# Gate units held behind attention and index scores, late expert units spread over the last stage, and the last outputs finished one by one

## The chip, the cores and the metric

The kernel runs on one core of a Trainium2 chip. The metric is device time in microseconds (us), the median of several executions. Names of engines here and below: PE is TensorE (matrix products), DVE is VectorE, ACT is ScalarE, POOL is GpSimd, SP is the engine whose queue issues most of the transfers.

## The reference

One layer of a streaming encoder for two groups of tokens that share weights: 256 tokens of a prompt, and 8 x 16 new tokens (the sample) with a cache of 256 past tokens each. In short:

```
mod = silu(c) W_ada + b_ada -> shift1, scale1, gate1, shift2, scale2, gate2
h = RMSNorm(x) * (1 + scale1) + shift1
P = h W_in, columns: [RWKV-7 | DSA attention + indexer | two branch gates]
branch A: RWKV-7 time mixing (16 heads of 64, a state update per token)
branch B: sparse attention: indexer I[t,s] = sum_h w[t,h] relu(q_idx[t,h].k_idx[s]),
          top-k admissible keys (k = 64 or 68 here), softmax over them
m = sigmoid(gA) * (oA W_pa) + sigmoid(gB) * (oB W_pb);  x = x + gate1 * (m W_out)
h2 = RMSNorm(x) * (1 + scale2) + shift2;  x = x + gate2 * PEER(h2)
PEER: 8 heads, 128 x 128 = 16384 experts, top 16 pairs of keys each;
      out = sum over chosen e of g_e gelu(h2 . u_e) v_e
```

All data is fp32 and D_MODEL is 1024.

## The kernel before

Products in fp32 are made of two halves: `hilo` rounds a tile to a high part (ACT, `wh`) and takes the difference as a low part (`wl`, on DVE or POOL), and a product is three matmuls, high x high, high x low and low x high. A weight tile is 512 KB (128 x 1024), is loaded by SP into a ring of four and split.

A tile scheduler sets the order on each engine; it starts from the order in which the program emits its steps. Engines run their own instructions in order and wait for one another by semaphores; `after(ins, other)` adds a wait by hand. The stages follow one another:

- **Front** (0 to some 735 us). `ORDER` is a string with a letter for each step: R is one of eight RWKV pairs (`rwkv_pair`), D a quarter of the attention heads (`dsa_quarter`), M a unit of the modulation (`mod_unit`), G one of sixteen gate units (`gate_unit`; a small g takes the low parts on POOL), I the indexer. A gate unit multiplies 24 matmuls of 128x384 (`tposp`, in the tile `mm`), takes a sigmoid on ACT and stores the result in DRAM (`d_401`) for later; nothing in the front waits for it. The indexer scores the sample (`index_s`: eight units of a key load `cki`, two matmuls into `dx`, a relu `rel` on ACT and a matmul into `bx`), then the prompt (`index_p`: matmuls into `dx`, then 8 rounds of max and replace on DVE per 128 tokens, `select`). An RWKV pair projects r, k and v (72 matmuls in `mm`), and then runs a chain of small matmuls and DVE steps. `attend_p` is the prompt's attention of a quarter, in two halves i of 128 tokens: scores `dx<-kT,qTp`, softmax, transposes of `se`, products with `vv`, and a store from `qr`.
- **Mix** (from some 733 us): the branches' outputs are loaded back from DRAM (`px`), split (`pbh`, `pbl`) and multiplied with the projections.
- **PEER choice**, then the dense half for the prompt: for 128 rows j of 128 experts, `dense_u` makes gelu(h2 . u) for all 256 prompt tokens, `weights` makes the gates (stored as `Wd`), and from 1326 us on the **v stage** multiplies them with `v` (`dense_v`, one unit per row j, all into the four outputs `bx`, `cp`, `dx`, `dx`). Every third unit is not split (`whole`: 8 matmul records on fp32 data). Rows 0 to 75 are kept in SBUF. Of the 52 late rows, 20 (76 to 95) are made beforehand and put into DRAM (`Ad`, read back as `gB`), 11 more are made beforehand and kept (`gA`), and the last 21 are made by `dense_u` inside the v stage when a place among the `gA` comes free. Late rows need their gates, loaded four rows at a time (`Ws`).
- The sample's experts are gathered row by row (`peer_sparse`, indirect transfers issued by POOL), spread by `pull(rate)` over the dense stages: a pull is two gathers, and `SR` holds the pulls per unit. A gather waits for the unit five before it (`pace`). All pulls are done by unit 122.
- **Tail**: `residual` multiplies each finished output by its gate, adds x and stores it.

Of the kernel before, what the change touches and what calls it, by code (L numbers as in the profile page):

```python
# [18 lines left out]
OP = mybir.AluOpType  # L19
# [154 lines left out]

PSB = {"mm": 2, "fx": 2, "bx": 1, "dx": 2, "cp": 1}
ALIAS = {"ix": "cp", "cs": "bx", "u": "fx"}
ORDER = "GGIggggRRDMMMGRMRDMRGMGMRMDGMMRRMGDMMMGGGMGGM"


N1, NW, NA, NB = 36, 76, 12, 20  # L180
SR, UR = (0.5, 0.4, 0.69), 0.5
S0, PH = 30, 4
WB, EB = (4, 4, 3), 5
UENG, VENG, GENG, VN = 'v', 'v', 'g', 3
SENG = 'gv'
# [7 lines left out]
class K:  # L193
# [76 lines left out]
            self.mm(p, lo[:, k, tok], wh, start=False, stop=(k == 7))  # L270
        return p

    def tposp(self, W, c, m, LT):

        hi, lo = LT
        p = self.ps([128, NT], tag="mm")[:m, :LT[0].shape[2]]
        cs = slice(c * 128, c * 128 + m)
        for k in range(8):
            wh, wl = W(k)
            self.mm(p, wh[:, cs], hi[:, k], start=(k == 0), stop=False)  # L280
# [686 lines left out]
    def index_p(self, qiT, kiT, wi):  # L967
        nc = self.nc
        out = []
        for i in range(2):  # L970
            n = 128 * (i + 1)
            sc = self.t([128, 276], tag="isc", bufs=2)[:, :256]
            for par in range(2):
                pr = slice(64 * par, 64 * par + 64)
                for c0 in range(0, 4, 2):
                    p = self.ps([128, 2, 256], tag="dx")
                    for j in range(2):
                        self.mm(p[:, j, :n], qiT[pr, c0 + j, i * 128:(i + 1) * 128], kiT[pr, 128:128 + n], tp=(64 * par, 0))
# [59 lines left out]
    def attend_p(self, u, qT, kT, vn, obT):  # L1038
        nc = self.nc
        for i in range(2):  # L1040
# [5 lines left out]
            for j in range(2):  # L1046
                for par in range(2):
                    pr = slice(64 * par, 64 * par + 64)
                    self.mm(ps2[par][:, j, :n], qT[pr, j, tok], kT[pr, j, 128:128 + n], start=(j == 0), stop=False, tp=(64 * par, 0))
            es = []  # L1050
            for par in range(2):
                p = ps2[par]
# [80 lines left out]
                nc.scalar.activation(dst, po[pr, :, :, par].rearrange("p b c t -> p c b t"), AF.Copy)  # L1133


    def gate_unit(self, u):

        W, _ = self.win(f"G{u}")
        g = self.t([128, NT], tag="gg", pool=self.fill)
        self.sigmoid(g, self.tposp(W, 0, 128, self.LT), self.hb[:, 16 + u:17 + u])  # L1140
        self.nc.sync.dma_start(self.gd[u], g)

    def parts(self, src, tag):
# [297 lines left out]
    def dense_u(self, j):  # L1441

        nc = self.nc
        u = self.expert(self.I["puT"][j].rearrange("p k e -> p (k e)"))
        p = self.ps([128, 256], tag="u")
        if j < N1:
            u = u.rearrange("p (k e) -> p k e", k=8)
            for k in range(8):
                self.mm(p, u[:, k], self.h2f[:, k], start=(k == 0), stop=(k == 7))
        else:  # L1450
            uh, ul = (x.rearrange("p (k e) -> p k e", k=8) for x in self.split(u, UENG[j % len(UENG)]))
            hi, lo = self.h2p
            for k in range(8):
                self.mm(p, uh[:, k], hi[:, k], start=(k == 0), stop=False)
                self.mm(p, uh[:, k], lo[:, k], start=False, stop=False)
                self.mm(p, ul[:, k], hi[:, k], start=False, stop=(k == 7))
        off = NW <= j < NW + NB
        g = self.kept(j) if j < NW else self.t([128, 256], tag="gO" if off else "gA", bufs=2 if off else NA, pool=self.late)
        nc.scalar.activation(g, p, AF.Gelu_apprx_tanh)  # L1459
        if off:  # L1460
            nc.sync.dma_start(self.Ad[j - NW], g)
        return g

    def dense_v(self, j, g, out, n):
        nc = self.nc
        v = self.expert(self.I["pv"][j * 128:(j + 1) * 128])
        whole = n % VN == 0 and n < 126
        if not whole:
            vh, vl = self.split(v, VENG[j % len(VENG)])
        if NW <= j < NW + NB:  # L1470
            g = self.t([128, 256], tag="gB", bufs=2)
            nc.sync.dma_start(g, self.Ad[j - NW])
# [12 lines left out]
        gh, gl = (self.t([128, 256], F32R, tag=tag, bufs=2) for tag in ("Gh", "Gl"))  # L1485
        self.hilo(gh, gl, g, "v")
        for i in range(2):
            tok = slice(i * 128, i * 128 + 128)
            for q, (l, r) in enumerate(((gh, vh), (gh, vl), (gl, vh))):
                for b in range(2):  # L1490
                    m = self.mm(out[i][b], l[:, tok], r[:, b * 512:(b + 1) * 512], start=(n == 0 and q == 0),
                                stop=(n == 127 and q == 2))
        self.vdone.append(m.ins.name)

    def weights_back(self, j):

        self.ws = self.t([128, 8, 4, 32], tag="Ws", bufs=2)
        self.nc.sync.dma_start(self.ws, self.Wd[:, :, j - NW:j - NW + 4].rearrange("c p a n -> p c a n"))

    def gate2(self, sp):  # L1500

# [5 lines left out]
    def residual(self, i, parts, g, x1):  # L1507

        nc = self.nc
        y = self.ring()  # L1510
        for b in range(2):
            cols = slice(b * 512, b * 512 + 512)
            nc.vector.tensor_tensor(y[:, cols], parts[b], g[:, cols], op=OP.mult)
            (nc.vector if i == 1 and b else nc.gpsimd).tensor_tensor(y[:, cols], y[:, cols], x1[:, cols], op=OP.add)  # L1514
            nc.sync.dma_start(self.O["y"][i * 128:(i + 1) * 128, cols], y[:, cols])

    def x1_rows(self, i):
# [40 lines left out]
    def run(self):  # L1558
        self.dense = False
        with ExitStack() as front:  # L1560
# [20 lines left out]
            with ExitStack() as s:  # L1581
                rw = self.open(s, "rw")
                self.pool = rw
                self.rwkv_head()
                ds, n = None, dict.fromkeys("RGD", 0) | {"M": 8}
                for x in ORDER:
                    if x == "I":
# [8 lines left out]
                    {"R": self.rwkv_pair, "M": self.mod_unit, "G": self.gate_unit, "D": self.dsa_quarter}[x](n[x])  # L1596
                    n[x] += 1
                self.nc.sync.dma_start(self.O["sh"], self.last)
            fh.close()
# [51 lines left out]

        def ahead(n):
            un[0] += UR
            if todo and un[0] >= 1 and (todo[0] < NW + NB or todo[0] < NW + NB + NA - 1):
                un[0] -= 1
                u = todo.pop(0)
                gs[u] = self.dense_u(u)
# [13 lines left out]
        self.weights_back(NW)  # L1671
        self.g2 = self.modrow(5, "fx")

        self.vdone = []
        for n, j in enumerate(order):
            self.pace = self.vdone[n - 5] if n > 4 else None
            pull(SR[2])
            while todo and sum(u >= NW + NB for u in gs) < NA - 1:
                u = todo.pop(0)
                gs[u] = self.dense_u(u)  # L1680
            self.dense_v(j, gs.pop(j) if j >= NW else self.kept(j), out, n)
            if n == 122:
                for _ in sparse:
                    pass
                self.residual(0, [self.acc[:, b * 512:b * 512 + 512] for b in range(2)], self.gate2(0), self.x1_rows(0))
                g, x1 = self.gate2(1), [self.x1_rows(i) for i in (1, 2)]
        for i in range(2):
            self.residual(1 + i, out[i], g, x1[i])

# [24 lines left out]
```

## Time and profile before

| | |
|---|---|
| Median of 3 runs | 1814.69 us (1809.4 to 1818.53) |
| The profiled execution | 1820.84 us |
| Its span in the trace | 1819.1 us |
| PE busy | 1722.2 us, 95% |
| DVE busy | 1353.9 us, 74% |
| Last matmul starts | 1809.62 us |

A profile row names the line, the engine, the operation and its tiles (output<-inputs), with start and duration in us, and in brackets how long the engine had idled and what it waited for. A row for a stretch gives its length, then the busy time of PE, PE's weight load, DVE, ACT and POOL, then the clock granted to PE (1.00 is full), the busy share of the DMA engines and GB/s. A busy PE is one that has a matmul under way, at whatever clock.

### The profile page before, as it was taken

To read this page: it belongs to the slowest core of one execution; us is meant where nothing else is said; L and a number is where in the kernel's file an instruction comes from. 1 tells how busy PE (TensorE), PEld (TensorE's weight loads), DVE (VectorE), ACT (ScalarE), POOL (GpSimd) and SP (SyncE) were. 2 spreads that over 40 slices of the span, in tenths; PEclk is the share of its full clock that TensorE was granted. 3 is DMA by queue.
4 is the path that set the end of the run, shared out by engine and by line. 5 is a ranking of instruction groups with operands and counts; after the bars stand their busy time and mean duration, and the time that the engine had idled before them with its cause. 6 is when DMAs were issued, how large, how long until landed. Compare 5 with 4: busy or idle time off the path is not lost. (4 is left out here: it accounts for less than half of the span.)

```text
span 1819.1 us, 33550 instructions
## 1 busy us (share of the span) xinstructions
PE 1722.2 (95%) x12576; PEld 1427.0 (78%) x12576; DVE 1353.9 (74%) x2942; ACT 701.7 (39%) x1411; POOL 687.8 (38%) x755
## 2 busy tenths in 40 slices
PE   6998899999999999999989999999998889999998
PEld 4986778877887877898878889999965556777765
DVE  3448867878677775455999999899957778777783
ACT  4532242333343333334322254488832223333332
POOL 1432232332233120024154446533355666555541
PEclk7998899999899998899999999999999999999999
DMA  8541373355354454655489989965489999999994
GB/s 289 161 129 44 90 255 114 102 172 159 118 193 133 124 198 164 226 181 170 151 326 327 339 312 364 380 236 184 170 303 379 393 366 374 347 382 355 341 342 150
DMA packets 181083, 434.11 MB, mean 239 GB/s; under 512 B 39348, under 2 KB 78388, under 8 KB 180920
## 3 DMA queue, kind: packets, MB, share of 16 engines
q1 hardware_dynamic: 144056, 297.73, 47.8%
q0 software_dynamic: 36864, 134.23, 19.8%
q8 instruction: 99, 1.62, 0.4%
q14 instruction: 64, 0.52, 0.1%
HBM read 401.65 MB, written 30.24 MB: 237 GB/s over the span
## 5 line engine op out<-in xcount | busy, mean ns | idle before, releaser
L231 DVE TENSOR_TENSOR wl<-w,wh 128x1024 fp32r<-128x1024 f32 (+1 forms) x274 | 343.9, 1258 | 140.3 <-ACT wh L227 77.2
L227 ACT ACTIVATE wh<-w 128x1024 fp32r<-128x1024 f32 (+1 forms) x282 | 296.0, 1053 | 203.9 <-PE mm L223 75.1
L1532 POOL DMA_INDIRECT raw<-in_pu,pe x128 | 162.4, 1269 | 173.2 <-PE dx L223 43.1
L223 PE MATMUL fx<-h2h,wh 128*128 128x256 f32 x736 | 215.4, 293 | 7.2 <-ACT wh L227 5.4
L223 PE MATMUL fx<-h2h,wl 128*128 128x256 f32 x736 | 212.3, 289 | 4.2 <-DVE wl L231 4.0
L1532 POOL DMA_INDIRECT raw<-in_pv,pe x128 | 168.8, 1319 | 124.1 <-PE dx L223 41.7
L223 PE MATMUL fx<-h2l,wh 128*128 128x256 f32 x736 | 209.3, 284 | 0.0
L1553 DVE SCALAR_TENSOR_TENSOR acc<-raw,dots,acc 128x1024 f32<-128x1024 f32 x127 | 164.9, 1298 | 10.5 <-DMA raw<-in_pv,pe 9.2
L1543 DVE SCALAR_TENSOR_TENSOR raw<-raw,sh 128x1024 f32<-128x1024 f32 x128 | 157.6, 1242 | 14.4 <-DMA raw<-in_pu,pe 14.2
L223 PEld LDWEIGHTS fx<-h2h,wh 128*128 128x128 f32 x736 | 139.9, 190 | 13.2 <-ACT wh L227 7.0
L223 PEld LDWEIGHTS fx<-h2h,wl 128*128 128x128 f32 x736 | 139.5, 190 | 7.7 <-DVE wl L231 5.9
L223 PEld LDWEIGHTS fx<-h2l,wh 128*128 128x128 f32 x736 | 140.0, 190 | 2.1 <-issue 1.7
L223 PE MATMUL fx<-h2f,w 128*128 128x256 f32 x576 | 128.6, 384 | 9.1 <-ACT G L1459 6.3
L223 PEld LDWEIGHTS fx<-h2f,w 128*128 128x128 f32 x576 | 109.8, 192 | 26.2 <-ACT G L1459 7.5
L223 PE MATMUL mm<-LTh,wh 128*128 128x384 f32 (+2 forms) x352 | 124.5, 354 | 1.6 <-ACT wh L227 1.0
L223 PE MATMUL mm<-LTh,wl 128*128 128x384 f32 (+2 forms) x352 | 123.2, 350 | 0.6 <-DVE wl L231 0.6
L223 PE MATMUL mm<-LTl,wh 128*128 128x384 f32 (+2 forms) x352 | 121.7, 346 | 1.1 <-POOL LTl L477 1.1
L223 PE MATMUL mm<-wh,LTh 128*128 128x256 f32 x336 | 99.1, 295 | 0.0
L223 PE MATMUL mm<-wl,LTh 128*128 128x256 f32 x336 | 98.3, 293 | 0.0
L223 PE MATMUL mm<-wh,LTl 128*128 128x256 f32 x336 | 98.1, 292 | 0.0
L1381 POOL TENSOR_TENSOR G<-G,wg 128x144 f32<-128x144 f32 (+1 forms) x64 | 54.4, 874 | 95.5 <-ACT wg L1378 95.5
L223 PEld LDWEIGHTS mm<-LTh,wh 128*128 128x128 f32 (+2 forms) x352 | 66.6, 189 | 10.1 <-issue 5.2
(557 smaller groups left out, 4157.5 us busy)
## 6 DMA issues: line engine op xcount, KB each, us to landing
w<-in_puT SPq DMA_DIRECT2D x128, 512.0 KB
w<-in_pv SPq DMA_DIRECT2D x128, 512.0 KB
w<-in_w_in SPq DMA_DIRECT2D x70, 512.0 KB
w<-in_w_ada SPq DMA_DIRECT2D x48, 512.0 KB
cKT<-in_cKT SPq DMA_DIRECT2D x32, 256.0 KB
cV<-in_cV SPq DMA_DIRECT2D x32, 256.0 KB
w<-in_w_pq SPq DMA_DIRECT2D x16, 512.0 KB
d<-wst SPq DMA_DIRECT2D x8, 832.0 KB
```

The lines of the kernel that those rows point to most:

```text
L223: return self.nc.tensor.matmul(out, l, r, start=start, stop=stop, skip_group_check=True, **kw)
L227: self.nc.scalar.activation(hi, src, AF.Copy)
L231: (self.nc.vector if eng == "v" else self.nc.gpsimd).tensor_tensor(lo, src, hi, op=OP.subtract)
L1381: (nc.vector if w is p else nc.gpsimd).tensor_tensor(g, g, w[:, :, c0:c1], op=OP.mult)
L1532: d = nc.gpsimd.indirect_dma_start(out=u, out_offset=None, in_=src, in_offset=bass.IndirectOffsetOnAxis(ap=e[:, j:j + 1], axis=0))
L1543: nc.vector.scalar_tensor_tensor(u, u, 1.0, h2, op0=OP.mult, op1=OP.mult, accum_out=dots[:, j:j + 1])
L1553: nc.vector.scalar_tensor_tensor(acc, v, dots[:, j:j + 1], acc, op0=OP.mult, op1=OP.add)
```

## The change

It has three parts.

1. The order of the front: `GGIggggRRD` becomes `GGIRgggggRD`, so the first RWKV pair comes ahead of the early gates, which are five, and one late gate is gone. The first matmul of each early gate waits for the first prompt score of the indexer (`held`). Gate units 14 and 15, the last two, wait for the last score matmul of the two halves of the latest attention quarter (`behind`).
2. The v stage: the 20 rows that go through DRAM are spread evenly over the 52 late rows (`OFF`) and no longer the first 20; the 11 others made beforehand are the first 11 of the rest (`AHEAD`), so the remaining 21 come between the others from the stage's start. `SR[2]` falls from 0.69 to 0.59, with a pull more per late u unit. `Ws` holds six rows, not four: 9 loads, not 13.
3. The tail: the last two units are multiplied by `finish_v`, one output after the other, and the adds of both last `residual` calls run on DVE.

```diff
-ORDER = "GGIggggRRDMMMGRMRDMRGMGMRMDGMMRRMGDMMMGGGMGGM"
+ORDER = "GGIRgggggRDMMMGRMRDMRGMGMRMDGMMRRMGDMMMGGMGGM"
-SR, UR = (0.5, 0.4, 0.69), 0.5
+SR, UR = (0.5, 0.4, 0.59), 0.5
+OFF = [j for j in range(NW, 128) if (j - NW + 1) * NB // (128 - NW) > (j - NW) * NB // (128 - NW)]
+AHEAD = sorted(OFF + [j for j in range(NW, 128) if j not in OFF][:NA - 1])
+LAST = 126
...
-    def tposp(self, W, c, m, LT):
+    def tposp(self, W, c, m, LT, behind=None):
...
+            m = self.mm(p, wh[:, cs], hi[:, k], start=(k == 0), stop=False)
+            if behind is not None and k == 0:
+                self.after(m, behind)
...
     def index_p(self, qiT, kiT, wi):
+        self.held = None
...
+                        m = self.mm(p[:, j, :n], qiT[pr, c0 + j, i * 128:(i + 1) * 128], kiT[pr, 128:128 + n], tp=(64 * par, 0))
+                        self.held = self.held or m
...
+                    m = self.mm(ps2[par][:, j, :n], qT[pr, j, tok], kT[pr, j, 128:128 + n], start=(j == 0), stop=False, tp=(64 * par, 0))
+            self.behind[14 + i] = m
...
+                    if x == "G":
+                        self.gate_unit(n[x], self.held if self.lo_pattern == "g" else self.behind.get(n[x]))
...
-        off = NW <= j < NW + NB
+        off = j in OFF
...
-            q = (j - NW) % 4
+            q = (j - NW) % 6
...
+        if n >= LAST:
+            return gh, gl, vh, vl
...
+    def finish_v(self, parts, out):
+
+        for i in range(2):
+            tok = slice(i * 128, i * 128 + 128)
+            for b in range(2):
+                for n, (gh, gl, vh, vl) in enumerate(parts):
+                    for q, (l, r) in enumerate(((gh, vh), (gh, vl), (gl, vh))):
+                        self.mm(out[i][b], l[:, tok], r[:, b * 512:(b + 1) * 512], start=False, stop=(n == len(parts) - 1 and q == 2))
...
-            (nc.vector if i == 1 and b else nc.gpsimd).tensor_tensor(y[:, cols], y[:, cols], x1[:, cols], op=OP.add)
+            (nc.vector if i else nc.gpsimd).tensor_tensor(y[:, cols], y[:, cols], x1[:, cols], op=OP.add)
...
-        gs, todo = {}, list(range(NW, 128))
+        gs, todo = {}, AHEAD + [j for j in range(NW, 128) if j not in AHEAD]
...
-            while todo and sum(u >= NW + NB for u in gs) < NA - 1:
+            while todo and sum(u not in OFF for u in gs) < NA - 1:
+                pull(SR[2])
                 u = todo.pop(0)
                 gs[u] = self.dense_u(u)
```

How the order of instructions moves is shown at three places. The first is PE in the indexer, before. `dx_913` to `dx_929` are the sample's score units, `bx_912` their sum; `mm_1254` is an early gate, `mm_1292` and `mm_1335` are the first two projections of RWKV pair 0.

```order
L223 MATMUL mm_1254<-LTh_168,wl_1250 128x384
L223 MATMUL mm_1292<-LTh_168,wh_1284 128x384
...
L223 MATMUL dx_921<-cki_922,qiTs_674 128x256
L223 MATMUL bx_912<-rel_918,qr_902 128x272
L223 MATMUL dx_921<-kiT_619,qiTs_674 128x16
...
L223 MATMUL mm_1335<-LTh_168,wh_1327 128x384
...
L223 MATMUL bx_912<-rel_926,qr_902 128x272
```

And after, PE at the same place; `mm_1238` is the third projection of pair 0, `dx_1015` holds the first prompt scores, `mm_1729` is the first of the five early gates.

```order
L226 MATMUL mm_1238<-LTh_168,wl_1231 128x384
L226 MATMUL dx_900<-wT_896,ce_898 128x128
L226 MATMUL dx_913<-cki_914,qiTs_674 128x256
...
L226 MATMUL dx_921<-cki_922,qiTs_674 128x256
L226 MATMUL dx_921<-kiT_619,qiTs_674 128x16
L226 MATMUL bx_912<-rel_918,qr_902 128x272
...
L226 MATMUL bx_912<-rel_966,qr_902 128x272
L226 MATMUL dx_1015<-kiT_619,qiTp_675 128x128 x2
L226 MATMUL mm_1729<-LTh_168,wh_1724 128x384
```

The projections of pair 0 now all stand ahead of the sample's scores, which follow one another with no gate or projection between, and the gates begin behind the first prompt scores.

The second place is the end of the front. On PE before, `dx_8764` and `dx_8809` are the last scores of the two halves of the last attention quarter; the gates 14 and 15 stand 20 and more rows ahead of the first.

```order
L223 MATMUL dx_8764<-kT_8217,qTp_8216 128x128 x2
...
L1068 MATMUL dx_8786<-cfirst,se_8774 128x128 x2
...
L1081 MATMUL dx_8803<-cfirst,ob_8801 128x128 x2
...
L223 MATMUL dx_8809<-kT_8217,qTp_8216 128x256 x2
...
L1068 MATMUL dx_8842<-cfirst,se_8827 128x128 x4
L223 MATMUL mm_9163<-pbh_9132,wh_9152 128x384
```

After, on PE, with the same scores as `dx_8799` and `dx_8844`; `mm_9037` is gate 14, `mm_9072` gate 15, `mm_9100` a modulation unit, `mm_9163` the first mix product.

```order
L226 MATMUL dx_8799<-kT_8252,qTp_8251 128x128 x2
...
L226 MATMUL mm_9037<-LTh_168,wh_9032 128x384
...
L226 MATMUL dx_8844<-kT_8252,qTp_8251 128x256 x2
...
L226 MATMUL mm_9072<-LTh_168,wh_9067 128x384
...
L226 MATMUL mm_9100<-w_9107,cst 32x256 x4
L226 MATMUL dx_8865<-vv_8253,set_8871 128x64 x4
...
L1089 MATMUL dx_8891<-cfirst,ob_8889 128x128 x2
L226 MATMUL mm_9163<-pbh_9132,wh_9152 128x384
```

Each gate now stands behind its scores and ahead of the later steps of the same half, and the attention's last transposes (`ob_8889`) stand ahead of the first mix product. SP's queue at the same place, before, where `d_402` takes the RWKV output and `d_403` the attention's:

```order
L662 DMA d_402<-sq_1611_8155 128x384
L1148 DMA px_9134<-d_402 128x768
L1148 DMA px_9138<-d_402 128x768
...
L1148 DMA px_9420<-d_403 128x768
L958 DMA d_403<-qr_8545 128x768
```

and after:

```order
L667 DMA d_402<-sq_1616_8190 128x384
L240 DMA w_9282<-in_w_proj_a 128x1024
...
L1149 DMA d_401<-gg_9071 128x384
L401 DMA d_102<-mr_9113 128x256
L963 DMA d_403<-qr_8580 128x768
L1156 DMA px_9134<-d_402 128x768
```

The loads `px` of the RWKV output stood ahead of the attention's store, and stand behind it now.

The third place is SP's queue at the start of the v stage, before:

```order
L1498 DMA Ws_15333<-d_11262 128x8x128
L1472 DMA gB_15449<-d_11263 128x256
L1472 DMA gB_15515<-d_11263 128x256
L1498 DMA Ws_15679<-d_11262 128x8x128
L1430 DMA w_15509<-in_pv 128x1024
```

and after:

```order
L1518 DMA Ws_15333<-d_11262 128x8x192
L1480 DMA gB_15622<-d_11263 128x256
L1480 DMA gB_15873<-d_11263 128x256
L1518 DMA Ws_15916<-d_11262 128x8x192
L1438 DMA w_15512<-in_pv 128x1024
L1438 DMA w_15540<-in_pv 128x1024
L1438 DMA w_15571<-in_puT 128x1024
```

Loads of `in_puT`, for the late u units, stand among those of `in_pv` from here on; before, the first came some fifty units later.

More of the change, by code (lines that the diff above doesn't have):

```diff
@@ L279, in tposp @@
             wh, wl = W(k)
-            self.mm(p, wh[:, cs], hi[:, k], start=(k == 0), stop=False)
+            m = self.mm(p, wh[:, cs], hi[:, k], start=(k == 0), stop=False)
+            if behind is not None and k == 0:
+                self.after(m, behind)
             self.mm(p, wh[:, cs], lo[:, k], start=False, stop=False)
@@ L977, in index_p @@
                     for j in range(2):
-                        self.mm(p[:, j, :n], qiT[pr, c0 + j, i * 128:(i + 1) * 128], kiT[pr, 128:128 + n], tp=(64 * par, 0))
+                        m = self.mm(p[:, j, :n], qiT[pr, c0 + j, i * 128:(i + 1) * 128], kiT[pr, 128:128 + n], tp=(64 * par, 0))
+                        self.held = self.held or m
                     for j in range(2):
@@ L1048, in attend_p @@
                     pr = slice(64 * par, 64 * par + 64)
-                    self.mm(ps2[par][:, j, :n], qT[pr, j, tok], kT[pr, j, 128:128 + n], start=(j == 0), stop=False, tp=(64 * par, 0))
+                    m = self.mm(ps2[par][:, j, :n], qT[pr, j, tok], kT[pr, j, 128:128 + n], start=(j == 0), stop=False, tp=(64 * par, 0))
+            self.behind[14 + i] = m
             es = []
@@ L1133, in attend_s, with gate_unit @@
                 nc.scalar.activation(dst, po[pr, :, :, par].rearrange("p b c t -> p c b t"), AF.Copy)
-    def gate_unit(self, u):
+    def gate_unit(self, u, behind=None):
         W, _ = self.win(f"G{u}")
         g = self.t([128, NT], tag="gg", pool=self.fill)
-        self.sigmoid(g, self.tposp(W, 0, 128, self.LT), self.hb[:, 16 + u:17 + u])
+        self.sigmoid(g, self.tposp(W, 0, 128, self.LT, behind), self.hb[:, 16 + u:17 + u])
         self.nc.sync.dma_start(self.gd[u], g)
@@ L1460, in dense_u @@
         if off:
-            nc.sync.dma_start(self.Ad[j - NW], g)
+            nc.sync.dma_start(self.Ad[OFF.index(j)], g)
         return g
@@ L1466, in dense_v @@
         v = self.expert(self.I["pv"][j * 128:(j + 1) * 128])
-        whole = n % VN == 0 and n < 126
+        whole = n % VN == 0 and n < LAST
         if not whole:
             vh, vl = self.split(v, VENG[j % len(VENG)])
-        if NW <= j < NW + NB:
+        if j in OFF:
             g = self.t([128, 256], tag="gB", bufs=2)
-            nc.sync.dma_start(g, self.Ad[j - NW])
+            nc.sync.dma_start(g, self.Ad[OFF.index(j)])
         if j >= NW:
-            q = (j - NW) % 4
+            q = (j - NW) % 6
             if q == 0 and j > NW:
@@ L1491, in dense_v @@
                     m = self.mm(out[i][b], l[:, tok], r[:, b * 512:(b + 1) * 512], start=(n == 0 and q == 0),
-                                stop=(n == 127 and q == 2))
+                                stop=False)
         self.vdone.append(m.ins.name)
+    def finish_v(self, parts, out):
[5 more added lines that the diff above has]
+                        self.mm(out[i][b], l[:, tok], r[:, b * 512:(b + 1) * 512], start=False, stop=(n == len(parts) - 1 and q == 2))
     def weights_back(self, j):
-        self.ws = self.t([128, 8, 4, 32], tag="Ws", bufs=2)
-        self.nc.sync.dma_start(self.ws, self.Wd[:, :, j - NW:j - NW + 4].rearrange("c p a n -> p c a n"))
+        self.ws = self.t([128, 8, 6, 32], tag="Ws", bufs=2)
+        n = min(6, 128 - j)
+        self.nc.sync.dma_start(self.ws[:, :, :n], self.Wd[:, :, j - NW:j - NW + n].rearrange("c p a n -> p c a n"))
     def gate2(self, sp):
@@ L1584, in run @@
                 self.rwkv_head()
+                self.behind = {}
                 ds, n = None, dict.fromkeys("RGD", 0) | {"M": 8}
@@ L1595, in run @@
                     x = x.upper()
-                    {"R": self.rwkv_pair, "M": self.mod_unit, "G": self.gate_unit, "D": self.dsa_quarter}[x](n[x])
+                    if x == "G":
+                        self.gate_unit(n[x], self.held if self.lo_pattern == "g" else self.behind.get(n[x]))
+                    else:
+                        {"R": self.rwkv_pair, "M": self.mod_unit, "D": self.dsa_quarter}[x](n[x])
                     n[x] += 1
@@ L1653, in ahead @@
             un[0] += UR
-            if todo and un[0] >= 1 and (todo[0] < NW + NB or todo[0] < NW + NB + NA - 1):
+            if todo and un[0] >= 1 and todo[0] in AHEAD:
                 un[0] -= 1
@@ L1672, in run @@
         self.g2 = self.modrow(5, "fx")
-        self.vdone = []
+        self.vdone, last = [], []
         for n, j in enumerate(order):
@@ L1677, in run @@
             pull(SR[2])
-            while todo and sum(u >= NW + NB for u in gs) < NA - 1:
+            while todo and sum(u not in OFF for u in gs) < NA - 1:
+                pull(SR[2])
                 u = todo.pop(0)
                 gs[u] = self.dense_u(u)
-            self.dense_v(j, gs.pop(j) if j >= NW else self.kept(j), out, n)
+            last.append(self.dense_v(j, gs.pop(j) if j >= NW else self.kept(j), out, n))
             if n == 122:
@@ L1686, in run @@
                 g, x1 = self.gate2(1), [self.x1_rows(i) for i in (1, 2)]
+        self.finish_v(last[LAST:], out)
         for i in range(2):
```

## The prediction

> **What bounds the kernel now.** I read the page first: busy times, then the slices.
>
> ```profile
> span 1819.1 us, 33550 instructions
> PE 1722.2 (95%) x12576; PEld 1427.0 (78%) x12576; DVE 1353.9 (74%) x2942; ACT 701.7 (39%) x1411; POOL 687.8 (38%) x755
> PE   6998899999999999999989999999998889999998
> PEclk7998899999899998899999999999999999999999
> ```
>
> TensorE (PE) is busy 95% of the span, so time can only come from stretches where it idles or runs at a lowered clock. A slice is 45.5 us. PE is low in slices 4 and 5 (136 to 227 us), where the clock drops too, in slice 21, and in slices 31 to 33 (1364 to 1501 us). The clock also drops in slices 16 and 17 (682 to 773 us), and in slice 11, which the change leaves alone. Next came the busy time of each engine by stretch, cut at those places and at the stages' ends.
>
> ```profile
> core 0: us, PE busy (x) PEld busy (x) DVE busy (x) ACT busy (x) POOL busy (x), PEclk, DMA share, GB/s
> 104.00:134.00 30.00, 30.00 (x154) 25.43 (x153) 10.48 (x22) 10.74 (x21) 5.25 (x17) 1.00 0.33 98
> 134.00:160.00 26.00, 26.00 (x156) 22.59 (x155) 20.34 (x57) 6.90 (x18) 8.46 (x23) 1.00 0.26 82
> 160.00:196.00 36.00, 24.55 (x115) 17.26 (x115) 32.80 (x127) 7.59 (x19) 4.51 (x9) 0.57 0.12 30
> 714.00:733.00 19.00, 17.10 (x94) 12.85 (x93) 10.03 (x27) 6.10 (x22) 3.94 (x4) 0.60 0.26 87
> 733.00:746.00 13.00, 12.06 (x58) 11.05 (x57) 5.94 (x8) 4.09 (x7) 0.00 (x0) 0.80 0.93 332
> 1326.00:1520.00 194.00, 171.80 (x583) 110.66 (x582) 138.69 (x182) 49.25 (x81) 121.28 (x105) 0.97 0.98 367
> 1520.00:1740.00 220.00, 215.26 (x1052) 163.11 (x1051) 171.55 (x212) 79.64 (x122) 119.33 (x93) 1.00 0.97 362
> 1740.00:1810.00 70.00, 70.00 (x254) 47.29 (x252) 40.18 (x49) 22.55 (x34) 14.71 (x11) 1.00 0.68 243
> ```
>
> Three places lose time, and the change touches all of them. From 160 to 196 VectorE (DVE) is full (32.80 of 36) while PE has little to do at 0.57 of its clock. From 714 to 733 PE works at 0.60. From 1326 to 1520 the transfers are at 0.98 and PE idles 22 us; afterwards PE is full, and in the last 70 us the transfers have room.
>
> **Part A, the early gates.** PE's own rows in the hole:
>
> ```profile
> 151.75 1.13 PE L223 MATMUL dx<-kiT,qiTp 64*128 64x256 f32 x4
> 165.44 2.07 PE L223 MATMUL dx<-kiT,qiTp 64*128 64x256 f32 x4
> 179.88 0.87 PE L569 MATMUL fx<-cfirst,sq 128*128 128x128 f32 x3 [3.33 <-DVE TL L686]
> 187.45 1.41 PE L223 MATMUL fx<-cfront,ra 128*128 128x2 f32 x6 [6.70 <-DVE ra L581]
> ```
>
> The same four matmuls take 1.13 us at 151.75 and 2.07 at 165.44, 1.83 times as long; the idle gaps wait for DVE. At full clock the 24.55 us would be 24.55 / 1.83 = 13.4, so the hole holds 36 - 13.4 = 22.6 us that independent matmuls could fill. [...]
>
> What can fill it is a gate unit, 24 matmuls of 128x384, and the projections of the next RWKV pair, 72 of them:
>
> ```profile
> 109.02 0.70 PE L223 MATMUL dx<-cki,qiTs 64*128 64x256 f32 x2
> 110.05 0.34 PE L223 MATMUL mm<-LTl,wh 128*128 128x384 f32 x1
> 112.70 0.34 PE L223 MATMUL mm<-LTl,wh 128*128 128x384 f32 x1
> 114.30 0.73 PE L223 MATMUL bx<-rel,qr 128*128 128x272 f32 x2
> 133.86 0.69 PE L223 MATMUL dx<-kiT,qiTp 64*128 64x128 f32 x4
> ```
>
> Between 110.05 and 112.70 lie 15 such starts: 0.177 us each, 4.25 a gate, 21 us for five. Before, four gates run ahead of and inside the sample index scores (109.02 to 133.86), so that the first prompt score comes at 133.86 and the long DVE selections after it fall into the hole. After, PE meets the sample scores bare: eight units of about 0.70 + 0.73 and a short one, some 13 us. The first prompt score then comes at about 118, the five gates (21 us) and pair 1's projections (72 x 0.177 = 12.7) stand beside the selections and pair 0's chain, and DVE's free time in 104 to 160 (30 - 10.48 + 26 - 20.34 = 25 us) is used. The matmuls are the same in number; the late gate that is one fewer is paid here. New is that a bare score unit waits for its own key load and its relu: bounded by 0 (all hidden) and by 25 - 13 = 12 us (a unit as slow as now, 24.84 / 8 = 3.1 us). I take 5, near the lower end, since those 3.1 us are mostly gate matmuls. Late next will be DVE again, with 63.6 us of work from 104 to 196, so I leave 4 us unfilled: 22.6 - 5 - 4, **about 14 us**, between 5 and 22.
>
> **Part B, the last gates.** Rows around the end of the front:
>
> ```profile
> 707.81 0.56 ACT L430 ACTIVATE gg<-mm,hb 128x384 f32<-128x384 f32 x1
> 723.88 0.38 ACT L1082 ACTIVATE qr<-dx 128x256 f32<-128x256 f32 x1 [2.13 <-PE dx L1081]
> 729.00 0.80 SPq L1148 DMA_DIRECT2D px<-d  x2
> 733.17 1.01 PE L223 MATMUL mm<-pbh,wh 128*128 128x384 f32 x2
> 745.36 0.32 SPq L958 DMA_DIRECT2D d<-qr  x1
> ```
>
> The last gates end at 707.81, before the slow stretch; after, both (8.5 us) and a mod unit stand inside it, so the chains that it consists of start some 8.5 us earlier and PE's work there costs nothing. Against that stands the SP queue: the loads px, at 729.00 now, come behind the attention's store d<-qr, at 745.36 now because mix matmuls stand ahead of its last steps on PE. Unhindered, the second half of the attention should take about as long as the steps from 723.88 to 733 and a little, so I put the store at 727 to 729 and the first mix matmul at 731 (733.17 now), with nothing of the attention left among the mix matmuls. Those run 733.17 to 746 now at a clock of 0.80; at full clock they need 12.06 x 0.80 = 9.6, 3.4 less. 2 + 3.4 = 5.4, **about 5 us**. Ends: 714 to 746 holds 17.10 x 0.60 + 12.06 x 0.80 = 19.9 us of full-clock work in 32, so at most 12 less; and 3 more if the store lands late.
>
> **Part C, the v stage.**
>
> ```profile
> w<-in_pv SPq DMA_DIRECT2D x122, 512.0 KB
> w<-in_puT SPq DMA_DIRECT2D x21, 512.0 KB
> Ws<-d SPq DMA_DIRECT2D x13, 512.0 KB
> gB<-d SPq DMA_DIRECT2D x20, 128.0 KB
> raw<-in_pu,pe POOLq DMA_INDIRECT x76
> raw<-in_pv,pe POOLq DMA_INDIRECT x76
> L223 PE MATMUL bx<-wh,Gh 128*128 128x512 f32 x16 | 9.1, 566 | 0.0
> L223 PE MATMUL bx<-w,G 128*128 128x512 f32 x8 | 4.1, 591 | 0.0
> L223 PE MATMUL bx<-w,gA 128*128 128x512 f32 x6 | 3.1, 591 | 0.0
> ```
>
> The first six rows are the loads from 1326 to 1810, the last three PE groups of the last 70 us: 16 split units have one such matmul each, the unsplit ones two, so 16 + 14 / 2 = 23 units in 70 us, 3.0 each. 128 such units and 21 late u units of about the same length are 149 x 3.0 = 447 us, against 484 now: PE could gain 37 at most. The transfers say less. 122 + 21 + 152 = 295 large ones are moved; about 31 of them (23 units, 8 gathers) in the last 70 us, so 264 in the first 414, 1.57 us each with Ws and gB among them. The gathers end at nearly the same unit after as before (76 / 0.59 - 21 = 108; 76 / 0.69 = 110), which leaves some 20 units, 60 us, with one transfer each: (295 - 20) x 1.57 + 60 = 492, **8 us slower**. For it, Ws and gB (13 x 0.5 + 20 x 0.125 = 9 MB, at 367 GB/s 25 us) now spread to the end: a third, 8 us, goes where transfers have room, and the 22 us that PE waits in the first 194 shrink as the u units stand there. [...] Between -8 and +37, nearer to the transfers' side as they stand at 0.97 in both stretches: **about 5 us**, range -8 to 15.
>
> **Part D, the tail.**
>
> ```profile
> 1809.62 0.63 PE L223 MATMUL dx<-wh,Gl 128*128 128x512 f32 x2
> 1809.67 0.69 DVE L1513 TENSOR_TENSOR raw<-bx,raw 128x512 f32<-128x512 f32 x1 [4.38 <-PE bx L223]
> 1810.44 4.15 POOL L1514 TENSOR_TENSOR raw<-raw,raw 128x512 f32<-128x512 f32 x3 [35.01 <-DVE raw L1513]
> 1812.07 1.40 DVE L1514 TENSOR_TENSOR raw<-raw,raw 128x512 f32<-128x512 f32 x1
> ```
>
> The last matmul ends at 1810.25 and the last add on POOL at 1814.59, 4.3 us later. After, outputs finish six matmuls (1.4 us) apart, and a multiply and an add of one output remain on DVE: 0.69 + 0.69 to 1.40 = 1.4 to 2.1. [...]
>
> **Sum.** 14 + 5 + 5 + 2.5 = 26.5 us. The profiled execution took 1820.84 (span 1819.1 and 1.7 around it), 6.2 above the median of 1814.69; 1814.69 - 26.5 = 1788.
>
> **Rivals.**
> 1. The v stage gives nothing or costs 8 (the transfers' sum above): 1793 to 1801. For it: 0.98 and 0.97. Against it: PE's 22 idle us lie in the very stretch that now gets other work.
> 2. The store ahead of px is late and B comes to 0 or -3: 1793 to 1796. For it: 745.36 now. Against it: what delays it there is gone.
> 3. Bare score units pace PE at 3.1 us, so that A falls to 5: 1797.
> 4. Slower: the late u loads stand in SP's one queue among the pv loads from the stage's start. If a u load waits for a buffer, the pv loads behind it wait, and the transfers fall from 0.98. The other parts give 21.5 and 9 more is needed to be noticed: the stage must lose 31 us in about 85 units with u units among them, 0.36 a unit, on 4.0 to 4.2. Against it: from 1520 to 1740 the same loads run mixed, at 0.97 with PE full. Time 1824 or more.
>
> **Chances and range.** My sum 0.55, rival 1 0.17, rival 2 0.10, rival 3 0.10, rival 4 0.05, something better (A and C near their ends, 1770) 0.03. A measurement tells 0.5% (9.1 us) from no change: faster is below 1805.6. Rivals 1 to 3 singly still lie below it; in pairs (1 and 3: 1805 to 1810) they don't, so 0.82 faster, 0.13 within, 0.05 slower. Low end: A 20, B 9, C 12, D 2.5 = 43.5, 1771. High end: rivals 1 and 3 together with D, 1808.
>
> **What would show it.** A: the first prompt score near 118 and a clock of 1.00 from 160 to 196. B: gates between the attention's scores, px no later than 729 less the gain of A, no clock of 0.60. C: PE idle in the stage's first 194 us well under 22, the transfers' share falling only in the last 60. D: last add within 2.1 us of the last matmul. Wrong it would be if the sample scores showed gaps on PE of over 1 us a unit, or if the transfers stayed at 0.98 with the stage still 484 long.

## The result, and the profile after

The changed kernel is slower: 1842.38 us (median of 4 runs, 1831.16 to 1849.27) against 1814.83 (4 runs) for the kernel before on the same chip, a ratio of 1.0141 with a 95% interval of 1.0097 to 1.0185. The prediction was 1788, faster, with a range up to 1808. The profiled execution took 1846.0. Its page, the same four lines as before:

```profile
span 1844.0 us, 33500 instructions
PE 1740.9 (94%) x12576; PEld 1433.4 (78%) x12576; DVE 1361.8 (74%) x2944; ACT 703.0 (38%) x1411; POOL 685.4 (37%) x753
PE   6999999999999999899999989999999999989998
PEclk8979989999999999899999999999999999999999
```

The low slices 4 and 5 are gone; slice 3 (92 to 138 us) has a low clock instead, and slice 17 (738 to 784 us) is low in both rows. PE has the same 12576 records but 18.7 us more busy time. In this trace PE is busy for 109.0 us at half clock, in the one before for 88.6 us, which by my estimate (half of the difference) makes up 10 of the 18.7; the rest I can't place. By stretch:

```profile
core 0: us, PE busy (x) PEld busy (x) DVE busy (x) ACT busy (x) POOL busy (x), PEclk, DMA share, GB/s
104.00:134.00 30.00, 28.94 (x91) 21.89 (x92) 10.59 (x27) 4.78 (x14) 4.54 (x10) 0.60 0.11 32
134.00:160.00 26.00, 26.00 (x151) 20.45 (x150) 23.68 (x87) 9.76 (x20) 5.54 (x3) 1.00 0.34 96
160.00:196.00 36.00, 35.04 (x265) 33.53 (x264) 30.94 (x81) 14.44 (x28) 17.35 (x29) 1.00 0.52 162
714.00:733.00 19.00, 18.69 (x226) 14.91 (x225) 12.22 (x40) 5.62 (x20) 4.20 (x4) 0.91 0.12 38
733.00:746.00 13.00, 12.30 (x81) 9.23 (x80) 6.79 (x14) 5.97 (x15) 0.00 (x0) 1.00 0.29 90
746.00:757.00 11.00, 2.38 (x18) 1.77 (x17) 1.41 (x3) 1.20 (x2) 0.00 (x0) 0.75 0.89 300
```

The hole from 160 to 196 is filled as forecast: 265 matmul records at full clock where 115 ran at 0.57. Two stretches pay. From 104 to 134 the clock is 0.60 and 91 records stand where 154 did; and from 746 to 757, where the mix should run, PE works 2.38 us of 11. The early rows on PE, with rows between left out:

```profile
106.51 1.19 PE L226 MATMUL dx<-cki,qiTs 64*128 64x256 f32 x2 [0.94 <-DMA cki<-in_cKI]
109.16 1.25 PE L226 MATMUL bx<-rel,qr 128*128 128x272 f32 x2
118.77 1.22 PE L226 MATMUL dx<-cki,qiTs 64*128 64x256 f32 x2
121.36 1.22 PE L226 MATMUL dx<-cki,qiTs 64*128 64x256 f32 x2
123.95 1.22 PE L226 MATMUL dx<-kiT,qiTp 64*128 64x128 f32 x4
```

A bare score unit takes 2.59 us (118.77 to 121.36), and its matmuls 1.22 and 1.25, where 0.70 and 0.73 were measured between gates. By the records PE has no gap there, so it is the lower clock, and not a wait for a key or a relu, that the unit's length shows. The first prompt score comes at 123.95: earlier than 133.86, later than the forecast 118. The end of the front, all engines (`gg` is the last gate, `mr` the modulation unit, `qr` the attention's output; `sq`, further below, is an RWKV pair's):

```profile
744.98 1.33 SPq L240 DMA_DIRECT2D w<-in_w_proj_a  x3
746.73 0.33 SPq L1149 DMA_DIRECT2D d<-gg  x1
747.15 0.38 SPq L401 DMA_DIRECT2D d<-mr  x1
750.13 0.32 SPq L963 DMA_DIRECT2D d<-qr  x1
752.86 0.79 SPq L1156 DMA_DIRECT2D px<-d  x2
756.18 1.68 ACT L230 ACTIVATE pbh<-px 128x768 fp32r<-128x768 f32 x2 [6.08 <-DMA px<-d]
757.08 1.01 PE L226 MATMUL mm<-pbh,wh 128*128 128x384 f32 x2 [7.39 <-ACT pbh L230]
```

The first mix product starts at 757.08 (733.17 before) after 7.39 us of idle PE. The v stage, in the same three lengths as before, from its own start at 1344:

```profile
1344.00:1538.00 194.00, 180.02 (x766) 128.66 (x765) 142.26 (x177) 58.55 (x94) 111.98 (x98) 0.97 0.97 361
1538.00:1758.00 220.00, 204.81 (x843) 143.56 (x842) 173.90 (x211) 67.64 (x103) 121.50 (x100) 0.98 0.96 362
1758.00:1828.00 70.00, 68.20 (x241) 45.24 (x242) 44.37 (x54) 25.95 (x39) 17.85 (x14) 1.00 0.79 279
```

PE idles 14.0 us in the first stretch (22.2 before), but 15.2 in the second (4.7). The tail:

```profile
1835.13 0.39 PE L226 MATMUL bx<-wh,Gl 128*128 128x512 f32 x1
1835.56 0.69 DVE L1533 TENSOR_TENSOR raw<-bx,raw 128x512 f32<-128x512 f32 x1 [4.32 <-PE bx L226]
1835.59 0.63 PE L226 MATMUL dx<-wh,Gl 128*128 128x512 f32 x2
1837.96 2.49 DVE L1534 TENSOR_TENSOR raw<-raw,raw 128x512 f32<-128x512 f32 x4
```

The four outputs get their last matmuls within 1.1 us of one another, so all four multiplies and adds still stand behind them: 4.2 us from the last matmul (1836.22) to the last add (1840.45), as before (4.3).

### The profile page after: what moved, and what is told of

Same layout as the page of the kernel before. It is cut to its first block, busy times and chain, and to the rows that moved or that the text cites. A ratio compares the mean times of both kernels' runs of the same rounds, so it can differ in the third digit from the quotient of the medians.

```text
span 1844.0 us, 33500 instructions
## 1 busy us (share of the span) xinstructions
PE 1740.9 (94%) x12576; PEld 1433.4 (78%) x12576; DVE 1361.8 (74%) x2944; ACT 703.0 (38%) x1411; POOL 685.4 (37%) x753
## 4 chain that ended last, share of the span: by engine, by line
PE 65%; DVE 14%; DMA 13%; issue 3%; POOL 2%; ACT 2%; SPq 0%; DVEq 0%; POOLq 0%; ACTq 0%
PE mm L226 23%; PE fx L226 15%; PE dx L226 11%; PE cp L226 7%; PE bx L226 7%; DMA w<-in_pv 2%; DVE raw L1563 2%; DMA raw<-in_pv,pe 2%; DVE acc L1573 2%; DMA raw<-in_pu,pe 2%; DVE wl L234 2%; DMA w<-in_w_ada 1%; ACT wh L230 1%; POOL raw L1552 1%; DVE psi L1293 1%
## 5 line engine op out<-in xcount | busy, mean ns | idle before, releaser
L1552 POOL DMA_INDIRECT raw<-in_pu,pe x128 | 156.4, 1222 | 171.0 <-DVE acc L1573 52.7
```

Source lines behind the costliest of these rows:

```text
L1552: d = nc.gpsimd.indirect_dma_start(out=u, out_offset=None, in_=src, in_offset=bass.IndirectOffsetOnAxis(ap=e[:, j:j + 1], axis=0))
```

## The experiments

Every ratio is to the kernel before, run beside it on the same chip, with its 95% interval.

**Each part alone.** The kernel before with one part of the change.

```diff
p_order: ORDER = "GGIRgggggRDMMM...GGMGGM", early gates wait for self.held
p_late:  gates 14 and 15 wait for self.behind[14 + i]
p_v:     OFF, AHEAD, SR[2] = 0.59 with pull(SR[2]), Ws of six rows
p_tail:  finish_v for the last two units, adds of residual on DVE
```

> The kernel before with the early part alone: the new order string and the early gates held behind the first prompt score; late gates, v stage and tail as before. Theory: this part loses time, since the sample's score units run bare at half the clock and pair 2 starts 12 us later in the trace of the change; the end of the last RWKV pair comes 6 to 14 us late, ratio 1.003 to 1.008. Rival: the hole at 160 to 196 us is filled and stays so, and the loss of the change comes from elsewhere; 5 to 14 us faster, ratio 0.992 to 0.997.

> The kernel before with gates 14 and 15 held behind the last attention scores, nothing else. Theory: the loads px land behind the attention's store and PE waits 7 us for them with nothing left to do, so this costs 6 to 12 us, ratio 1.003 to 1.007. Rival: the wait for px was caused by the early part's shift, and here the gates in the slow stretch save 3 to 8 us, ratio 0.996 to 0.998.

> The kernel before with the v stage's part alone (20 stored rows spread, late u units from the start, rate 0.59 with a pull per late u unit, gates six rows at a time). Theory: the transfers bound the stage in both, and fewer transfers are left free at the end, so the stage is 4 to 10 us longer, ratio 1.002 to 1.006. Rival: as predicted, 5 us shorter, ratio 0.997.

> The kernel before with the tail's part alone (last two units output by output, last adds on DVE). Both theories: 1 to 2.5 us faster, ratio 0.9985 to 0.9995; in the trace the last add ends 1.4 to 2.1 us behind the last matmul.

| | median us (runs) | ratio |
|---|---|---|
| p_order | 1836.35 (4) | 1.0109 (1.0069 to 1.0150) |
| p_late | 1828.11 (9) | 1.0046 (1.0019 to 1.0074) |
| p_v | 1817.78 (10) | 0.9998 (0.9971 to 1.0025) |
| p_tail | 1816.01 (10) | 0.9999 (0.9975 to 1.0022) |

The four add up to 1.0152, the whole is 1.0141: the loss is that of the two front parts. p_v shows where its own part's gain went:

```profile
1313.00:1507.00 194.00, 180.25 (x779) 129.78 (x778) 144.65 (x179) 59.09 (x96) 112.35 (x99) 0.98 0.99 366
1507.00:1727.00 220.00, 207.88 (x857) 146.52 (x856) 176.34 (x216) 69.57 (x106) 125.31 (x102) 0.98 0.98 368
1727.00:1797.00 70.00, 69.78 (x252) 46.90 (x251) 40.98 (x49) 24.18 (x36) 15.79 (x12) 1.00 0.70 246
```

PE works 457.9 us of these 484, before 457.1 (171.80 + 215.26 + 70.00). The idle time moved from the first stretch to the second, and the transfers stay at 0.98 and more in both. From the first product into `bx` to the last matmul the stage takes 477.3 us, before 478.5.

**The late gates.** My first theory was that px comes late because it stands behind the attention's store d<-qr on SP; rivals were the second gate, and the weights and the stores of the gates.

```diff
l_act: p_late, and the last quarter's store
-        nc.sync.dma_start(self.obd[:, 2 * u:2 * u + 2], ob)
+        (nc.scalar if u == 3 else nc.sync).dma_start(self.obd[:, 2 * u:2 * u + 2], ob)
l_one: p_late, only gate 14 waits
s_late: the kernel before, only the store of gate 15 waits for the last scores
```

> The late gates held behind the last attention scores, and the attention's last store issued from ACT's queue, so that SP's loads px do not stand behind it. If the wait for px is what the held gates cost: the idle 7 us of PE before the first mix product go, ratio 0.997 to 1.001. Rival (the mix products wait for the attention on PE itself, or px for its memory): ratio 1.004 to 1.006 as with the store on SP.

> Only gate 14 is held, behind the scores of the first half; gate 15 is free, the store on SP. In SP's queue px then stands ahead of the store. If the store's place is what costs: ratio 0.997 to 1.001. Rival (what costs is that the gates delay the attention's steps on PE): ratio 1.002 to 1.004, about half of both gates.

> The kernel before, with gate 15's store to DRAM alone held behind the last score of the attention's second half; PE's order is as before. Theory (the loads px reuse memory of the gate tiles and wait until the last gate's store has landed, 5.4 to 6.1 us after its issue): px is issued 5 to 6 us after that store and first mix product 2 to 4 us later than 9 us behind the RWKV store. Rival (px waits for the RWKV store or for PE alone): px 4.6 us after the store d<-sq as before, whatever the gate's store does.

Measured: l_act 1.0067 (1.0044 to 1.0089), l_one 1.0071 (1.0043 to 1.0098), s_late one run of 1818.27 beside a median of 1815.11, which is too little to tell a change from none; s_late is there for its trace. l_act's queues:

```profile
725.69 1.33 SPq L237 DMA_DIRECT2D w<-in_w_proj_a  x3
727.86 0.39 SPq L398 DMA_DIRECT2D d<-mr  x1
730.84 0.34 ACTq L960 DMA_DIRECT2D d<-qr  x1
733.52 0.80 SPq L1151 DMA_DIRECT2D px<-d  x2
```

The store d<-qr is on another queue, and px still comes 5.66 us after d<-mr, as in the changed kernel (747.15 to 752.86, 5.71). So the place behind d<-qr was not the cause, and the first theory fell. s_late, whose store stands behind no weight loads:

```profile
727.86 0.33 SPq L1144 DMA_DIRECT2D d<-gg  x1
729.87 0.80 SPq L1153 DMA_DIRECT2D px<-d  x2
```

Here px follows the store after 2.0 us. In the built programs px waits for the semaphores of d<-sq, d<-gg and d<-mr, not for that of d<-qr (in s_late for some others too). The reason is memory: px takes the bytes from 100640 to 103711 of a partition, the unit's mr those from 102592 to 103615, and gg begins at 103616. The traces have the landings: in the changed kernel d<-mr lands at 752.80 and px is issued at 752.86, in l_act at 733.45 and 733.52, in s_late d<-gg at 729.73 and px at 729.87. So px comes when the late gate's and modulation unit's stores have landed, and behind three 512 KB weight loads that takes 5.7 us, alone 2.0. Other memory for gg and mr wasn't tried.

In p_late the first mix product comes 18.8 us after the last d<-sq and PE idles 7.40 us ahead of it; before it comes 9.1 us after. These 9.7 us are about the size of the loss (0.46%, 8 us). l_one doesn't fit as well: in its trace the first mix product comes 12.6 us after d<-sq, but its ratio is no better than p_late's. That trace is of an execution of 1816.33, 11 us below l_one's median, so where l_one loses its time stays open.

**The early gates.** Four theories: the bare score units cost it; the number of early gates (a late gate is missing at the end) does; pair 1, now behind the gates, does; pair 0 ahead of the gates does. The string is what changes, and with `held` the early gates wait for the first prompt score.

```diff
before  "GGIggggRRDMMM...GGGMGGM"
o_free  "GGIRgggggRDMMM...GGMGGM"  without held: gates stand between the score units
o_gate  "GGIRggggRDMMM...GGGMGGM"  held
o_three "GGIRgggRDMMM...GGGGMGGM"  held
g_five  "GGIgggggRRDMMM...GGMGGM"  not held
g_three "GGIgggRRDMMM...GGGGMGGM"  not held
o_rr5   "GGIRRgggggDMMM...GGMGGM"  held
o_rr4   "GGIRRggggDMMM...GGGMGGM"  held
h_only  before's string, held
```

> The kernel before with the new order string, but the five early gates not held (they stand between the sample's score units again); late gates, v stage and tail as before. Theory 1 (the loss of the early part is the bare score units at half clock, 10 us): that goes, so this is 8 to 12 us faster than the early part with its hold, ratio to before 1.000 to 1.006. Theory 2 (the loss is that pair 1 and the chains behind it start later, and that the late gate is missing where the chains end): little changes, ratio 1.008 to 1.012.

> The early part with its hold, but with four early gates, so that the late gate stays where it was; late gates, v stage and tail as before. Theory 1 (bare score units): the score units are as bare, ratio 1.008 to 1.011 as with five. Theory 2 (the fifth early gate shifts all chains by 4 us and leaves the chain-bound end of the front without that filler): 6 to 12 us of the loss go, ratio 1.003 to 1.007.

> Pair 0 ahead of the early gates, three early gates held behind the first prompt score, four in the late group; v stage and tail as before. With five held gates the ratio was 1.0109, with four 1.0042. Theory (each early gate costs 6 us or more): 0.996 to 1.000. Rival (the rest of the loss is the bare score units and pair 0's place): 1.003 to 1.006.

> The kernel before with one gate unit moved: five early gates, not four, and two in the late group, not three; pairs, holds, v stage and tail as before. Theory (a gate moved from the late group to the early one puts 4 us ahead of all chains and leaves the chain-bound end of the front without that filler): 5 to 12 us slower, ratio 1.003 to 1.007. Rival (where a gate stands does not matter by itself): 0.998 to 1.002.

> The kernel before with one gate unit moved the other way: three early gates, four in the late group. Theory (as for five early gates, the other way): 3 to 10 us faster, ratio 0.994 to 0.998, since PE's rows in the hole at 160 to 196 us stay as they are and all chains start 4 us earlier. Rival: 0.998 to 1.002, or slower if the early gates were the cover of the score units.

> The early part of the change with both first pairs ahead of the five held gates, two gates in the late group as in the change; late gates not held, v stage and tail as before. On PE the sample's score units then stand between pair 1's projections, and the gates behind the first prompt score. Theory E (the early part loses because pair 1 stands behind the gates: its chain and all behind it start later, and nothing covers the score units): most of the 20 us come back or more, ratio 0.992 to 1.003. Theory F (pair 0 ahead of the gates, or the hold itself, is what costs further on): 1.007 to 1.012.

> As the one before, with four early gates and three in the late group. Theory E: 0.992 to 1.003. Theory F: 1.004 to 1.010. If the missing late gate costs by itself, this one is 4 to 8 us faster than that with five.

> The order string of before with its four early gates held behind the first prompt score, nothing else. PE then meets the score units bare, the gates, and only then the projections of pairs 0 and 1. Theory E (pairs late): slower than the early part of the change, both chains start some 17 us of gate matmuls later, ratio 1.008 to 1.015. Theory F, with pair 0's place as the cost: 1.000 to 1.005.

| | ratio | | ratio |
|---|---|---|---|
| o_free | 1.0133 (1.0112 to 1.0154) | g_three | 1.0102 (1.0075 to 1.0129) |
| o_gate | 1.0042 (1.0017 to 1.0068) | o_rr5 | 1.0121 (1.0077 to 1.0166) |
| o_three | 1.0145 (1.0083 to 1.0207) | o_rr4 | 1.0108 (1.0073 to 1.0144) |
| g_five | 1.0012 (0.9985 to 1.0038) | h_only | 1.0048 (1.0014 to 1.0081) |

All four theories fell as the one cause. Without bare units it is no better (o_free), and held gates alone cost 0.5% (h_only). The four runs of o_three spread from 1831 to 1854, so its size is unclear. The number of gates has no order: five cost nothing without pair 0 (g_five), three cost 1.0% (g_three). Pair 1 ahead of the gates doesn't mend it (o_rr5, o_rr4), and pair 0 ahead cost 0.4% in one version and 1.0% and more in the others. None of the four explains these numbers by itself.

**The order behind.** What these versions may have in common is that the scheduler orders the whole front anew; it was counted for one pair. From the first D on, p_order and g_five are written word for word alike; yet of their 3528 PE instructions there, each stands on average 26 places from where it stands in the other (counted in the built programs; 6 places on DVE). So the next three kernels hold that later order by hand, to the end of the front: `PIN` is a table of the order in one built program, and each instruction is put behind the one before it in the table, on all five engines.

```diff
+        for a, b in zip(seq, seq[1:]):        # seq: PIN, engine by engine
+            self.tc.add_manual_dep(traced[b], traced[a].name, ...)
p_pin: p_order, from the first D on in the order of g_five
o_pin: o_gate, from the first D on in the order of the kernel before
g_pin: g_five, from the first D on in the order of p_order
```

> The front's new order with held early gates (ratio 1.0109 by itself), but every instruction that is written from the first D on, on each of the five engines, is held in the order in which it stands when five early gates stand ahead of both pairs (that version 1.0012, the same text from the first D on). The front's first part keeps its new order. Theory H: the scheduler weaves the later pairs, quarters and gates otherwise once the first 200 us differ, and that weave is where the early gain is lost; then the ratio falls to 1.003 or below (about 1805 to 1821 us), and the ends of pairs 2 to 7 come no later than before. Rival K: the state that the new first part leaves (pair 1 late, weights late) is what costs; then the ratio stays at 1.008 to 1.014 with any order behind it.

> Pair 0 ahead of four held gates (1.0042 by itself), and from the first D on the order of the kernel before on every engine. Theory H: 0.990 to 1.000, the filled hole is kept. Rival K: about 1.004 or worse, 1.002 to 1.010.

> The reverse: five early gates ahead of both pairs (1.0012 by itself), and from the first D on the order that the scheduler made for the new string (1.0109). Theory H: the loss comes with the order, 1.006 to 1.015. Rival K: the loss stays away, 0.998 to 1.004.

| | median us (runs) | ratio | same first part, the scheduler's own order |
|---|---|---|---|
| p_pin | 1818.18 (12) | 0.9990 (0.9972 to 1.0007) | p_order 1.0109 |
| o_pin | 1813.8 (12) | 0.9974 (0.9952 to 0.9996) | o_gate 1.0042 |
| g_pin | 1835.91 (6) | 1.0097 (1.0066 to 1.0128) | g_five 1.0012 |

That settles it. With the first part kept, the other order behind takes 1.2% away (p_pin); with the first part of g_five, p_order's order behind brings 0.85% of loss (g_pin). The loss of part A goes with the order of the steps behind, which are written alike in p_order and g_five. o_pin is the one version that beats the kernel before, by 0.26%, 4.7 us; its interval ends just below 1, and among so many versions that is weak.

Where it shows is read from two traces, of executions of 1832.55 us (p_order) and 1821.22 (p_pin), which are 11.3 us apart; by the ratios the two kernels differ by some 22, so the traces show about half. First p_order's SP queue, and the matmul that waits for its load,

```profile
202.41 0.34 SPq L237 DMA_DIRECT2D w<-in_w_ada  x1
225.46 0.32 SPq L690 DMA_DIRECT2D d<-TX  x1
233.40 0.94 SPq L237 DMA_DIRECT2D w<-in_w_ada  x2
239.03 0.96 PE L223 MATMUL mm<-w,cst 128*32 128x256 f32 x2 [4.57 <-DMA w<-in_w_ada]
```

and p_pin's:

```profile
206.74 0.35 SPq L239 DMA_DIRECT2D w<-in_w_ada  x1
229.80 0.32 SPq L699 DMA_DIRECT2D d<-TX  x1
230.70 0.91 SPq L239 DMA_DIRECT2D w<-in_w_ada  x2
```

In both, one load of the modulation unit's weights goes ahead of d<-TX, pair 1's store, which waits for its chain. The next two stand 7.9 us behind d<-TX in p_order, after ten other transfers, and 0.9 us behind it with the held order. The row of 196 to 240 in p_order, and then in p_pin:

```profile
196.00:240.00 44.00, 38.70 (x499) 30.34 (x500) 30.36 (x84) 13.09 (x33) 9.22 (x11) 0.99 0.37 108
```

```profile
196.00:240.00 44.00, 43.12 (x548) 34.51 (x546) 29.57 (x82) 13.43 (x35) 11.23 (x13) 1.00 0.35 98
```

PE idles 5.3 us there in the one and 0.9 in the other. In the other pair of kernels this row shows less: g_pin idles 3.7 us, g_five 2.9. The second place: the stores d<-sq at the end of pairs 2, 3 and 7, and `mm` alone (projections, gates, modulation) between the first two of them, in p_order and then in p_pin:

```profile
399.49 0.33 SPq L664 DMA_DIRECT2D d<-sq  x1
472.76 0.59 SPq L664 DMA_DIRECT2D d<-sq  x1
739.30 0.33 SPq L664 DMA_DIRECT2D d<-sq  x1
400.00:473.30 73.30, 35.71 (x208) 26.51 (x207) 0.00 (x0) 4.78 (x14) 1.00 0.51 156
```

```profile
398.16 0.33 SPq L673 DMA_DIRECT2D d<-sq  x1
462.82 0.42 SPq L673 DMA_DIRECT2D d<-sq  x1
727.81 0.33 SPq L673 DMA_DIRECT2D d<-sq  x1
398.60:463.20 64.60, 32.82 (x171) 24.05 (x169) 0.00 (x0) 3.52 (x10) 1.00 0.54 164
```

Pair 2 ends 1.3 us apart in the two, pair 3 9.9, pair 7 11.5. In p_order PE puts 37 more `mm` matmuls between the two stores, so pair 3's chain has more work ahead of it on PE; from 350 to 500 PE idles 2.5 us in p_order and 1.6 in p_pin, so a row of busy time hardly shows it, and the ends of the pairs do.

This place goes with the order whatever the first part is. From pair 2's store to pair 3's, the traces in p_order's order take 73.3 us (p_order), 71.2 (g_pin) and 72.2 (the changed kernel), with 208 `mm` matmuls; those in the other order take 64.7 (p_pin) and 64.5 (g_five), with 171, and the kernel before 64.6. PE idles less than 1 us there in each of these traces, so what stands ahead of the store on PE sets the length. The end of pair 7 is less firm by itself: before, p_tail and p_v have the same order in the front, and it lies at 724, 722 and 715 us in them.

What stays open: which other places of the order cost how much; whether the order behind is all of the loss of the other strings in the table, which wasn't tried; and what the v stage adds, which `PIN` doesn't hold. From the first product into `bx` to the last matmul it takes 482 us in p_order's trace and 484 in g_pin's, 479 in those of p_pin and g_five.

## Why the prediction was wrong

**Part A, forecast 14 us gained; measured 1.09% lost by itself, some 20 us.** The step that failed is the first one, not written out: that what is gained at 196 is still there at 735. I treated the later front as shifted, while the scheduler lays it out anew, which the order of the built program would have shown. With a later order held that costs nothing by itself, the same first part stands at 0.9990 (p_pin), which can't be told from no change, and the one with four early gates at 0.9974 (o_pin), 5 us. So the term was mis-sized too, in two steps. The bare score units were put at 13 us and a cost of 5 on top; from 103.17 to the first prompt score at 123.95 they take 20.8 (other matmuls, `fx`, stand among them), so the cost was at most 7.8, inside its bounds of 0 and 12. Of it 0.94 us is a wait for a key, as I had named it; most of the rest comes with PE's clock (0.50 from 106.5 on), which I had not. And "late next will be DVE" was right but priced at 4: DVE had done 63.6 us of work in the 92 us from 104 to 196 and does 65.2 now (10.59 + 23.68 + 30.94). Its gain is 1.6 us, and the chains go through DVE (in the hole before, PE waited 3.33 and 6.70 us for it). That PE's filled hole was mostly work done ahead of need fits this; no run shows it by itself. The clock of 1.00 from 160 to 196 came as forecast and proved nothing about the end.

**Part B, forecast 5 us gained; measured 0.46% lost, 8 us.** From 714 to 746 the clock of 0.60 and 0.80 is gone (0.91 and 1.00), which was the expected gain; but the mix now begins behind idle PE, and from 746 to 757 the clock is 0.75. The step that failed is the wait on the SP queue: I named d<-qr as what px would stand behind and put it at 727 to 729. px waits for the stores of the very gate and unit that were moved late, and these came behind three weight loads. Rival 2 had the right queue and the wrong store, and its bound of -3 was too small.

**Part C, forecast 5; measured 0.9998, so within 5 us of nothing.** Rival 1. PE idle fell in the first 194 us as forecast, to 14, and came back in the next 220. The sign that I had named as disproof is there: the transfers at 0.98 with the stage as long as before. That they bound the stage is argued from this share alone. No run separates the spread of Ws and gB, the larger Ws and the new rate; together they were worth nothing that could be measured. Rival 4, late loads blocking the queue, didn't happen (p_v's transfers stood at 0.99 and 0.98 in its first two stretches).

**Part D, forecast 2.5; measured 0.9999 (0.9975 to 1.0022), which can't tell 2.5 from nothing; the tail's rows show 0.1.** No run shows the term of 2.5, which is my estimate from the rows before (4.3 us less 1.4 to 2.1, 2.2 to 2.9): what the runs showed is 4.2 us from the last matmul to the last add in the changed kernel, and no measurable gain in p_tail. The step that failed is "outputs finish six matmuls (1.4 us) apart". `finish_v` writes them so, but the rows show bx, cp and the two dx finishing in turn: the scheduler put them back side by side, and the order of the built program would have shown it.

**Sum and rivals.** Rival 1 came true for part C and rival 2 in part for B, but no rival had the front slower than before. All slower cases had been put into the v stage, at a chance of 0.05, because each front term was argued from a local hole. A slip besides: by their own terms rivals 1 and 3 together give 1802 to 1810, not 1805 to 1810.

## What to carry to other kernels

Where a scheduler sets the order, a change at the front of a stage can be two changes: the one that you wrote, and a new order for all that follows (here 1.0109 with both, 0.9990 with the first alone). Hold the later order fixed to see the first alone, before judging it. Count a filled hole on the busiest engine only as far as the chain that ends the stage moves (here 160 to 196 was filled to 35.04 us of 36 at full clock, and the changed kernel took 1.41% longer): look at the ends of that chain (here eight stores) and at the engine that it goes through. When work is moved late, follow its stores as well as its matmuls: what comes next may need the memory that they free (here px came 5.71 us after d<-mr).

## What the hardware showed

In the changed kernel PE's granted clock fell to 0.50 with no gap on PE above 0.94 us from 92 to 124. The scores took 0.70 us at 103.17 and 1.19 at 106.51, behind that gap of 0.94, and the records then follow one another without any gap up to 123.95, at this lower clock, which the trace has from 106.47 to 130.36:

```profile
103.17 0.70 PE L226 MATMUL dx<-cki,qiTs 64*128 64x256 f32 x2
...
110.00:120.00 10.00, 10.00 (x26) 6.71 (x25) 3.91 (x9) 1.19 (x3) 1.30 (x3) 0.50 0.07 21
```

It is a stretch of few matmuls (26 records in 10 us; from 96 to 103, at a clock of 1.00, there are 42 in 7). Why the clock fell is not shown: the records of matmuls overlap (one that starts at 118.77 ends at 119.99, the next starts at 119.78), so short waits between them may not show. And a store that was waited for 2.0 us alone (s_late) was waited for 5.7 us behind 1.5 MB of loads on the same queue (the changed kernel, l_act); what makes the difference is not shown.
